# Packing both parts of a split activation into one 512-column matmul, with the halves added at the exit from PSUM

## The chip, the cores and the metric

One NeuronCore of a Trainium2 chip runs the whole program. The metric is the device time of one execution in microseconds (us), as the median of several executions. Three runs of the kernel before took 2057.48, 2062.37 and 2063.44 us. The profiler's names of the engines are used throughout: PE is the tensor engine's matmul, PEld its load of the stationary operand, DVE the vector engine, ACT the scalar engine, POOL the GpSimd engine, SP the engine whose queue issues the loads from memory.

## The reference, cut to what matters

Two blocks of two layers each run over 256 context tokens and 256 latent tokens of width 1024. Each layer has a mixer (an mLSTM with two gated side paths in the first block, attention in the second), an output projection with a gated residual, and a feed-forward part. Where the change acts, this is computed:

```python
x = x + g1 * (y_x @ w_out[l])                          # output projection, residual
x = x + g2 * swiglu(rmsnorm(x, norm2_g[l]) * (1.0 + sc2) + sh2, w_gu[l], w_down[l])

def swiglu(h, w_gu, w_down):
    gate, up = jnp.split(h @ w_gu, 2, axis=-1)
    return (jax.nn.silu(gate) * up) @ w_down
```

All of it is in float32. In the first layer of each block the context tokens go the same way as the latent ones; in the last layer of each block only the latent tokens go on.

## The kernel before, in words

The residual stream lies in eight tiles `xT[k]` of 128 channels by 512 tokens (columns 0 to 255 are context, `CTX`; 256 to 511 are latents, `LAT`). A float32 product is made of three matmuls of a faster kind: a weight W is split in `whi` + `wlo` (an ACT copy at L392, a DVE subtraction at L397), an activation x in `aH` + `aL` (in the feed-forward part `hH` + `hL`), and W.T x is taken as whi·xH + whi·xL + wlo·xH. `mm3` (L411 to L413) issues these three, each with a stationary 128x128 tile of weights and 256 or 512 moving columns (tokens), and all three add up in the same columns of one PSUM bank, a tile of 512 float32 columns per partition. `accA` loops `mm3` over the eight (or 6 and 5) tiles of input channels. In this text the three matmuls for one tile of channels are called a triple.

Products of 512 tokens are those of the feed-forward parts that carry both streams (f0 with d0 in the first block, f2 with d2 in the second; d is the down projection), apart from a few at their heads and tails that go stream by stream (`order`). Products of 256 tokens are all output projections (`part`, called by `out_early`, `out_proj`, `out_stream` and `early_stream`), both parts of the feed-forward for latents alone (f1, d1, f3, d3), and those heads and tails. The products of the input projections are not touched.

What leaves PSUM: in a feed-forward part an ACT Silu reads the gate product `pg` (L557), a DVE multiplication reads the up product `pu` (L558), then the hidden tile is split (ACT and DVE, L378 and L379). In f1 and f3 the first two pairs of products take an input that is not yet normed ("raw", 258 columns) and leave by their own way. An output projection `po` or down projection `pd` leaves by one DVE instruction, x += g * product (`residual`, L454).

The order on each engine is worked out at build time by a scheduler that simulates readiness and follows priorities; on the chip each engine runs its list in order. Weight tiles go through three sets of buffers (five within a feed-forward part), PSUM tiles of products through three banks (five in f1 and f3). Beside the products DVE computes the modulation vectors of later layers, one dot product of 1024 elements per partition at a time (`junk`, L165), paced by `work`: one for each pair of products in f1, none in f3.

## Time and profile before

| what | value |
|---|---|
| runs, us | 2057.48, 2062.37, 2063.44 (median 2062.37) |
| span of the profiled execution, us | 2055.1 (its own time is not listed apart from the runs; the median lies 7.3 above the span) |
| PE busy | 2010.6 us, 98% |
| PEld busy | 1784.5 us, 87% |
| DVE busy | 1545.2 us, 75% |
| ACT busy | 924.5 us, 45% |
| POOL busy | 85.7 us, 4% |
| DMA, mean | 158 GB/s |
| chain that ended last | PE 89%, DVE 6%, ACT 2% |
| mean granted TensorE clock | 0.994 |

A row of PE is pipelined: a matmul's record is longer than the distance to the next one, so durations of PE records don't add up, and the pace is read from how many matmuls start in a stretch. In the rows of groups, "x" is a count, then come the busy time in us and the mean of one in ns. The stages in time: start and first mixer to 266 us, output projections 222 to 311, f0 with d0 to 690, second mixer to 858, f1 with d1 to 1045, attention and its output projections to 1277, f2 with d2 to 1640, attention and its output projection to 1860, f3 with d3 to the end.

### The profile page before, as it was taken

To read this page: it belongs to the slowest core of one execution; us is meant where nothing else is said; L and a number is where in the kernel's file an instruction comes from. 1 tells how busy PE (TensorE), PEld (TensorE's weight loads), DVE (VectorE), ACT (ScalarE), POOL (GpSimd) and SP (SyncE) were. 2 spreads that over 40 slices of the span, in tenths; PEclk is the share of its full clock that TensorE was granted. 3 is DMA by queue.
4 is the path that set the end of the run, shared out by engine and by line. 5 is a ranking of instruction groups with operands and counts; after the bars stand their busy time and mean duration, and the time that the engine had idled before them with its cause. 6 is when DMAs were issued, how large, how long until landed. Compare 5 with 4: busy or idle time off the path is not lost.

```text
span 2055.1 us, 34137 instructions
## 1 busy us (share of the span) xinstructions
PE 2010.6 (98%) x13196; PEld 1784.5 (87%) x13196; DVE 1545.2 (75%) x3105; ACT 924.5 (45%) x1612; POOL 85.7 (4%) x103
## 2 busy tenths in 40 slices
PE   8999999999999899999999999999999999999999
PEld 3798779888888799999998789888888889999999
DVE  6997789987898768987877667777653487788554
ACT  4324544222322346744556675322222266666443
POOL 0000010000001000200100002000000200001000
PEclk9999999999999999999999999999999999999999
DMA  7532265678766332576651015446752231216554
GB/s 295 181 103 92 97 232 176 211 248 295 235 216 198 111 102 94 170 263 212 202 171 61 22 41 186 154 149 223 260 170 71 70 112 64 73 54 224 182 157 134
DMA packets 98182, 324.22 MB, mean 158 GB/s; under 512 B 11418, under 2 KB 14234, under 8 KB 98020
## 3 DMA queue, kind: packets, MB, share of 16 engines
q1 hardware_dynamic: 98020, 322.04, 47.7%
q8 instruction: 104, 1.70, 0.3%
q14 instruction: 58, 0.48, 0.1%
HBM read 320.95 MB, written 1.05 MB: 157 GB/s over the span
## 4 chain that ended last, share of the span: by engine, by line
PE 89%; DVE 6%; ACT 2%; DMA 1%; issue 1%; SPq 0%; POOL 0%; ACTq 0%; POOLq 0%; DVEq 0%
PE pg L411 6%; PE pd L411 6%; PE pd L413 6%; PE pd L412 6%; PE pu L413 6%; PE pg L412 6%; PE pu L412 6%; PE pg L413 6%; PE pu L411 6%; PE pin L411 5%; PE pin L413 5%; PE pin L412 5%; PE pov L1223 2%; PE ptq L1127 2%; DVE wlo L397 1%; PE po L411 1%
## 5 line engine op out<-in xcount | busy, mean ns | idle before, releaser
L392 ACT CAST whi<-wraw 128x1024 fp32r<-128x1024 f32 (+2 forms) x443 | 429.5, 973 | 797.0 <-PE pu L412 188.9
L397 DVE TENSOR_TENSOR wlo<-wraw,whi 128x1024 fp32r<-128x1024 f32 (+2 forms) x443 | 502.5, 1138 | 155.0 <-ACT whi L392 152.3
L165 DVE CUSTOM_DVE_ANT_0 junk<-mw,cv,modb 128x1024 bf16<-128x1024 f32 x272 | 349.6, 1285 | 51.3 <-DMA mw<-in_modw 45.2
L411 PE MATMUL pd<-hH,whi 128*128 128x256 f32 (+1 forms) x748 | 245.4, 328 | 0.0
L412 PE MATMUL pd<-hL,whi 128*128 128x256 f32 (+1 forms) x748 | 245.1, 328 | 0.0
L413 PE MATMUL pd<-hH,wlo 128*128 128x256 f32 (+1 forms) x748 | 244.8, 327 | 0.0
L411 PE MATMUL pg<-aH,whi 128*128 128x256 f32 (+1 forms) x704 | 233.8, 332 | 0.3 <-ACT aH L374 0.3
L413 PE MATMUL pu<-aH,wlo 128*128 128x256 f32 (+1 forms) x704 | 233.5, 332 | 0.3 <-DVE wlo L397 0.3
L412 PE MATMUL pg<-aL,whi 128*128 128x256 f32 (+1 forms) x704 | 233.6, 332 | 0.0
L412 PE MATMUL pu<-aL,whi 128*128 128x256 f32 (+1 forms) x704 | 233.2, 331 | 0.0
L411 PE MATMUL pu<-aH,whi 128*128 128x256 f32 (+1 forms) x704 | 233.2, 331 | 0.0
L413 PE MATMUL pg<-aH,wlo 128*128 128x256 f32 (+1 forms) x704 | 233.2, 331 | 0.0
L412 PEld LDWEIGHTS pd<-hL,whi 128*128 128x128 f32 x748 | 142.2, 190 | 12.2
L411 PEld LDWEIGHTS pd<-hH,whi 128*128 128x128 f32 x748 | 142.4, 190 | 12.0
L413 PEld LDWEIGHTS pd<-hH,wlo 128*128 128x128 f32 x748 | 142.2, 190 | 12.0
L411 PE MATMUL pin<-whi,aH 128*128 128x256 f32 x512 | 150.0, 293 | 1.4 <-ACT aH L374 1.1
L412 PE MATMUL pin<-wlo,aH 128*128 128x256 f32 x512 | 148.0, 289 | 0.0
L413 PE MATMUL pin<-whi,aL 128*128 128x256 f32 x512 | 147.2, 289 | 0.3 <-DVE aL L375 0.2
L411 PEld LDWEIGHTS pg<-aH,whi 128*128 128x128 f32 x704 | 133.7, 190 | 13.2 <-ACT aH L374 0.5
L413 PEld LDWEIGHTS pu<-aH,wlo 128*128 128x128 f32 x704 | 133.7, 190 | 13.1 <-DVE wlo L397 0.5
L413 PEld LDWEIGHTS pg<-aH,wlo 128*128 128x128 f32 x704 | 133.8, 190 | 12.6
L412 PEld LDWEIGHTS pg<-aL,whi 128*128 128x128 f32 x704 | 133.8, 190 | 12.5
(339 smaller groups left out, 4150.8 us busy)
## 6 DMA issues: line engine op xcount, KB each, us to landing
wraw<-in_wgu SPq DMA_DIRECT2D x176, 512.0 KB, 4.4
mw<-in_modw SPq DMA_DIRECT2D x168, 512.0 KB, 4.2
wraw<-in_win SPq DMA_DIRECT2D x92, 512.0 KB, 3.5
wraw<-in_wdn SPq DMA_DIRECT2D x64, 384.0 KB, 3.5
wraw<-in_wout SPq DMA_DIRECT2D x47, 512.0 KB, 3.5
wraw<-in_wdn SPq DMA_DIRECT2D x64, 320.0 KB, 3.4
mn<-in_modn SPq DMA_DIRECT2D x18, 512.0 KB, 5.6
mn<-in_modw SPq DMA_DIRECT2D x6, 512.0 KB, 7.3
```

Source lines behind the costliest of these rows:

```text
L165: r = nc.vector.tensor_tensor_reduce(out=junk, in0=w, in1=self.cv[s], scale=1.0, scalar=self.mb_t[:, 2 * b + l, j:j + 1], op0=ALU.mult, op ...
L392: nc.scalar.copy(out=hi[:, :n], in_=raw[:, :n])
L397: nc.vector.tensor_tensor(out=lo[:, :n], in0=raw[:, :n], in1=hi[:, :n], op=ALU.subtract)
L411: mm(out=out, lhsT=wh, rhs=xh, start=start, stop=False)
L412: mm(out=out, lhsT=wh, rhs=xl, start=False, stop=False)
L413: mm(out=out, lhsT=wl, rhs=xh, start=False, stop=stop)
L1127: nc.tensor.transpose(out=pt[:, h, :], in_=a.bitcast(F32).rearrange("p e d -> p (e d)"), identity=self.ident)
L1223: nc.tensor.matmul(out=po[64 * b:64 * b + 64, e // 2, :], lhsT=vN[:, kc, 64 * g:64 * g + 64], rhs=u["PT"][:, kc, :], start=kc == 0, stop=k ...
```

## The change

`aH[k]` and `aL[k]` become the two halves of one tile `aP[k]` (128 x 2 x 512), `hH` and `hL` of one tile `hP`. For products of 256 tokens a new function `accP` takes, for each tile of channels, one matmul of 512 columns (whi against both parts, side by side in the PSUM tile: xH in columns 0 to 255, xL in 256 to 511) and one of 256 columns (wlo against xH, added to columns 256 to 511). For the last tile of channels the two change places. So the PSUM tile holds two halves whose sum is the product, and each way out of PSUM adds them: `residual` does its DVE instruction twice, once per half, and the feed-forward's exit copies the second half on ACT, adds the first on DVE, and goes on from SBUF. Raw pairs, the very first pair of f0 and f2, and products of 512 tokens stay as they were.

```diff
-        self.aH = [g.tile([128, T], F32R, name=f"aH{k}") for k in range(KT)]
-        self.aL = [g.tile([128, T], F32R, name=f"aL{k}") for k in range(KT)]
+        self.aP = [g.tile([128, 2, T], F32R, name=f"aP{k}") for k in range(KT)]
+        self.aH, self.aL = [[a[:, e, :] for a in self.aP] for e in range(2)]
...
+    def accP(self, out, w, xs, first=True, last=True):
+        mm = self.nc.tensor.matmul
+        n = len(xs)
+        for k, x in enumerate(xs):
+            q = slice(128 * k, 128 * k + 128)
+            big = lambda stop: mm(out=out.rearrange("p (e t) -> p e t", e=2), lhsT=w[0][:, q], rhs=x, start=first and k == 0, stop=stop)
+            small = lambda: mm(out=out[:, 256:512], lhsT=w[1][:, q], rhs=x[:, 0, :], start=False, stop=False)
+            if last and k == n - 1:
+                small()
+                big(True)
+            else:
+                big(False)
+                small()
...
     def residual(self, j, ps, cols, gains):
...
-                r = nc.vector.scalar_tensor_tensor(out=self.xT[j][:, a:b], in0=ps[:, a - c0:b - c0],
-                                                   scalar=gains[s][:, j:j + 1], in1=self.xT[j][:, a:b],
-                                                   op0=ALU.mult, op1=ALU.add)
-                self.fence = r.ins
+                for h in range(2 if c1 - c0 == 256 else 1):
+                    r = nc.vector.scalar_tensor_tensor(out=self.xT[j][:, a:b], in0=ps[:, 256 * h + a - c0:256 * h + b - c0],
+                                                       scalar=gains[s][:, j:j + 1], in1=self.xT[j][:, a:b],
+                                                       op0=ALU.mult, op1=ALU.add)
+                    self.fence = r.ins
...
     def part(self, p, w, ks, cols, first, last):
...
-            self.mm3(p[:, :c1 - c0], w[0][:, q], w[1][:, q], self.aH[k][:, c0:c1], self.aL[k][:, c0:c1],
-                     first and n == 0, last and n == len(ks) - 1)
+            self.accP(p, [a[:, q] for a in w], [self.aP[k][:, :, cols[0]:cols[1]]], first and n == 0, last and n == len(ks) - 1)
...
+                    packed = n == 256 and not raw and (i > 0 or hf > 0)
+                    if packed:
+                        for p, w in zip((pg, pu), ws[i]):
+                            self.accP(p, w, [a[:, :, c0:c1] for a in self.aP])
...
+                    elif packed:
+                        t1, t2 = (sg[:, 256:], h[:, 256:]) if both else [fp.tile([128, 256], F32, tag=nm, name=nm) for nm in ("rg", "ru")]
+                        nc.scalar.copy(out=t1, in_=pg[:, 256:])
+                        nc.vector.tensor_tensor(out=sg[:, :n], in0=pg[:, :n], in1=t1, op=ALU.add)
+                        nc.scalar.activation(out=sg[:, :n], in_=sg[:, :n], func=AF.Silu)
+                        nc.scalar.copy(out=t2, in_=pu[:, 256:])
+                        nc.vector.tensor_tensor(out=h[:, :n], in0=pu[:, :n], in1=t2, op=ALU.add)
+                        nc.vector.tensor_tensor(out=h[:, :n], in0=h[:, :n], in1=sg[:, :n], op=ALU.mult)
...
     def down(self, dns, colsets, gains, hs, pace, skew, after=None):
...
+            packed = c1 - c0 == 256
...
+                if packed:
+                    self.accP(p, ws[j, n], [x[:, :, c0:c1] for x in h], *ends)
```

The change moves instructions too, since the scheduler's list follows from the costs it simulates. Three places show what the lists look like.

PE, in f1, the last two tiles of channels of one up product, before (the numbers behind `aH` and `aL` are those of the tiles of channels):

```order
L411 MATMUL pu<-aH_95,whi 128x256
L412 MATMUL pu<-aL_103,whi 128x256
L413 MATMUL pu<-aH_95,wlo 128x256
L411 MATMUL pu<-aH_96,whi 128x256
L412 MATMUL pu<-aL_104,whi 128x256
L413 MATMUL pu<-aH_96,wlo 128x256
```

and now, with the first tile of the next gate product:

```order
L432 MATMUL pu<-aP_95,whi 128x512
L433 MATMUL pu<-aP_95,wlo 128x256
L433 MATMUL pu<-aP_96,wlo 128x256
L432 MATMUL pu<-aP_96,whi 128x512
L432 MATMUL pg<-aP_89,whi 128x512
L433 MATMUL pg<-aP_89,wlo 128x256
```

Three matmuls of 256 columns became one of 512 and one of 256. Over the whole program the list of PE has 1528 matmuls fewer.

DVE, in f1, before (`wlo` is the split of a weight tile for a later product, `hf` the product of gate and up, `hL` its low part, `junk` a dot product for a later layer's modulation):

```order
L558 TENSOR_TENSOR hf<-pu,sg 128x256
L397 TENSOR_TENSOR wlo<-wraw,whi 128x1024
L379 TENSOR_TENSOR hL_8932<-hf,hH_8921 128x256
L397 TENSOR_TENSOR wlo<-wraw,whi 128x1024
L558 TENSOR_TENSOR hf<-pu,sg 128x256
L397 TENSOR_TENSOR wlo<-wraw,whi 128x1024
L379 TENSOR_TENSOR hL_8933<-hf,hH_8922 128x256
```

and now, over about the same work:

```order
L580 TENSOR_TENSOR hf<-pu,ru 128x256
L397 TENSOR_TENSOR wlo<-wraw,whi 128x1024
L581 TENSOR_TENSOR hf<-hf,sg 128x256
L577 TENSOR_TENSOR sg<-pg,rg 128x256
L397 TENSOR_TENSOR wlo<-wraw,whi 128x1024
L379 TENSOR_TENSOR hP_8560<-hf,hP_8560 128x256
L580 TENSOR_TENSOR hf<-pu,ru 128x256
L581 TENSOR_TENSOR hf<-hf,sg 128x256
L397 TENSOR_TENSOR wlo<-wraw,whi 128x1024
L379 TENSOR_TENSOR hP_8561<-hf,hP_8561 128x256
```

Each pair of products has two more DVE instructions, the additions at L577 and L580, and each waits for an ACT copy of the other half (`rg`, `ru`). The splits of the weights stand about as far ahead as before.

DVE, where the latents' output projection of the first layer overlaps the norm of the context (`xn` and `aL` or `aP` are that norm's tiles, `xT` the residual), before:

```order
L373 SCALAR_TENSOR_TENSOR xn<-xT_83,modA_107,npb 128x256
L373 SCALAR_TENSOR_TENSOR xn<-xT_84,modA_107,npb 128x256
L454 SCALAR_TENSOR_TENSOR xT_85<-po,mod_105,xT_85 128x256
L397 TENSOR_TENSOR wlo<-wraw,whi 128x1024
L375 SCALAR_TENSOR_TENSOR aL_101<-xn,mod_105,aH_93 128x256
L375 SCALAR_TENSOR_TENSOR aL_102<-xn,mod_105,aH_94 128x256
L373 SCALAR_TENSOR_TENSOR xn<-xT_85,modA_107,npb 128x256
L373 SCALAR_TENSOR_TENSOR xn<-xT_86,modA_107,npb 128x256
L454 SCALAR_TENSOR_TENSOR xT_86<-po,mod_105,xT_86 128x256
L397 TENSOR_TENSOR wlo<-wraw,whi 128x1024
```

and now:

```order
L373 SCALAR_TENSOR_TENSOR xn<-xT_85,modA_99,npb 128x256
L373 SCALAR_TENSOR_TENSOR xn<-xT_86,modA_99,npb 128x256
L471 SCALAR_TENSOR_TENSOR xT_84<-po,mod_97,xT_84 128x256
L375 SCALAR_TENSOR_TENSOR aP_95<-xn,mod_97,aP_95 128x256
L375 SCALAR_TENSOR_TENSOR aP_96<-xn,mod_97,aP_96 128x256
L471 SCALAR_TENSOR_TENSOR xT_84<-po,mod_97,xT_84 128x256
L397 TENSOR_TENSOR wlo<-wraw,whi 128x1024 x4
L471 SCALAR_TENSOR_TENSOR xT_85<-po,mod_97,xT_85 128x256 x2
L397 TENSOR_TENSOR wlo<-wraw,whi 128x1024
L471 SCALAR_TENSOR_TENSOR xT_86<-po,mod_97,xT_86 128x256 x2
```

Each residual takes two instructions, and four splits of weights that stood between the norm's instructions now come behind them in a row.

## Rows read from the trace of the kernel before

**Rows 1.** The page, busy time by engine (us, share of the span, instructions).

```profile
span 2055.1 us, 34137 instructions
...
PE 2010.6 (98%) x13196; PEld 1784.5 (87%) x13196; DVE 1545.2 (75%) x3105; ACT 924.5 (45%) x1612; POOL 85.7 (4%) x103
```

**Rows 2.** Stretches of steady matmuls: busy us (count) by engine, clock, DMA share, GB/s.

```profile
340.00:640.00 300.00, 300.00 (x1324) 248.17 (x1323) 260.59 (x389) 83.54 (x108) 3.32 (x2) 1.00 0.73 239
1320.00:1620.00 300.00, 300.00 (x1325) 248.46 (x1324) 172.40 (x245) 79.94 (x105) 4.84 (x4) 1.00 0.52 168
...
900.00:980.00 80.00, 80.00 (x669) 80.00 (x669) 60.37 (x91) 36.20 (x57) 0.00 (x0) 1.00 0.65 215
...
1900.00:2040.00 140.00, 140.00 (x1172) 140.00 (x1171) 74.75 (x95) 60.80 (x89) 0.00 (x0) 1.00 0.57 174
```

**Rows 3.** Groups of PE by shape, whole span: the first matmul of each 256-column triple.

```profile
L411 PE MATMUL pd<-hH,whi 128*128 128x256 f32 x440 | 125.5, 285 | 0.0
...
L411 PE MATMUL pg<-aH,whi 128*128 128x256 f32 x384 | 109.1, 284 | 0.3 <-ACT aH L374 0.3
L411 PE MATMUL po<-aH,whi 128*128 128x256 f32 x376 | 108.8, 293 | 0.7 <-ACT aH L949 0.5
...
L411 PE MATMUL pg<-rawH,whi 128*128 128x258 f32 x32 | 9.2, 289 | 0.0
...
L411 PE MATMUL po<-aH,w 128*128 128x256 f32 x8 | 2.2, 280 | 0.0
```

**Rows 4.** Groups of DVE and ACT by shape, whole span: the exits from PSUM of 256 columns.

```profile
L454 DVE SCALAR_TENSOR_TENSOR xT<-pd,mod,xT 128x256 f32<-128x256 f32 x80 | 36.5, 479 | 37.9 <-PE pd L413 37.9
...
L454 DVE SCALAR_TENSOR_TENSOR xT<-po,mod,xT 128x256 f32<-128x256 f32 x48 | 22.8, 477 | 16.0 <-PE po L413 15.7
...
L511 DVE TENSOR_TENSOR rg<-pg,rb 128x256 f32<-128x256 f32 x4 | 1.7, 414 | 0.0
...
L1241 ACT COPY oN<-pto 128x256 f32<-128x256 f32 x16 | 6.0, 375 | 6.4 <-PE pto L1238 6.3
```

**Rows 5.** Groups of DVE by shape in f1, from 900 to 980 us.

```profile
L397 DVE TENSOR_TENSOR wlo<-wraw,whi 128x1024 fp32r<-128x1024 f32 x24 | 29.4, 1223 | 11.8 <-ACT whi L392 11.7
L165 DVE CUSTOM_DVE_ANT_0 junk<-mw,cv,modb 128x1024 bf16<-128x1024 f32 x14 | 17.9, 1281 | 0.2
L558 DVE TENSOR_TENSOR hf<-pu,sg 128x256 f32<-128x256 f32 x15 | 6.3, 421 | 5.8 <-PE pu L413 5.8
L379 DVE TENSOR_TENSOR hL<-hf,hH 128x256 fp32r<-128x256 f32 x14 | 5.8, 418 | 0.0
```

**Rows 6.** Stretches at the ends of output projections, columns as in rows 2.

```profile
290.00:311.00 21.00, 18.82 (x152) 18.39 (x152) 20.80 (x38) 12.22 (x21) 6.13 (x6) 1.00 0.71 243
835.00:858.00 23.00, 20.84 (x171) 20.37 (x170) 20.75 (x35) 15.73 (x31) 12.22 (x12) 1.00 0.67 219
...
1250.00:1280.00 30.00, 28.64 (x231) 27.75 (x231) 27.09 (x49) 18.03 (x28) 6.61 (x7) 1.00 0.62 215
1830.00:1860.00 30.00, 26.77 (x201) 25.48 (x201) 23.43 (x60) 19.34 (x40) 5.53 (x6) 0.94 0.28 97
```

**Rows 7.** The chain that ended last, residuals on it: start us, length us.

```profile
1265.78 0.40 DVE xT L454
...
1274.54 0.40 DVE xT L454
...
1844.38 0.21 PE po L412
...
1851.87 0.48 DVE xT L454
...
1860.14 0.40 DVE xT L454
...
2051.12 0.48 DVE xT L454
```

More of the change, by code (lines that the diff above doesn't have):

```diff
@@ L453, in residual @@
             if a < b:
-                r = nc.vector.scalar_tensor_tensor(out=self.xT[j][:, a:b], in0=ps[:, a - c0:b - c0],
-                                                   scalar=gains[s][:, j:j + 1], in1=self.xT[j][:, a:b],
-                                                   op0=ALU.mult, op1=ALU.add)
-                self.fence = r.ins
+                for h in range(2 if c1 - c0 == 256 else 1):
[3 more added lines that the diff above has]
+                    self.fence = r.ins
     def part(self, p, w, ks, cols, first, last):
-        c0, c1 = cols
         for n, k in enumerate(ks):
             q = slice(128 * k, 128 * k + 128)
-            self.mm3(p[:, :c1 - c0], w[0][:, q], w[1][:, q], self.aH[k][:, c0:c1], self.aL[k][:, c0:c1],
-                     first and n == 0, last and n == len(ks) - 1)
+            self.accP(p, [a[:, q] for a in w], [self.aP[k][:, :, cols[0]:cols[1]]], first and n == 0, last and n == len(ks) - 1)
     def out_early(self, src, cols, ks):
@@ L531, in ffn @@
                 tg = "" if both else str(hf) + "_"
-                hH = [fp.tile([128, w_h], F32R, tag=f"hH{tg}{i}", name=f"hH{i}") for i in range(HALF)]
-                hL = [fp.tile([128, w_h], F32R, tag=f"hL{tg}{i}", name=f"hL{i}") for i in range(HALF)]
-                hs.append((hH, hL))
+                hP = [fp.tile([128, 2, w_h], F32R, tag=f"hP{tg}{i}", name=f"hP{i}") for i in range(HALF)]
+                hs.append(hP)
                 ws = {}
@@ L543, in ffn @@
                     xs, m, cs = ((rH, rL), 258, (0, 258)) if raw else ((self.aH, self.aL), n, cols)
-                    if i == 0 and hf == 0:
+                    packed = n == 256 and not raw and (i > 0 or hf > 0)
+                    if packed:
+                        for p, w in zip((pg, pu), ws[i]):
+                            self.accP(p, w, [a[:, :, c0:c1] for a in self.aP])
+                    elif i == 0 and hf == 0:
                         self.accA([pg[:, :m], pu[:, :m]], ws[i], xs, cs)
@@ L558, in ffn @@
                         nc.vector.tensor_tensor(out=h[:, :n], in0=pu[:, :n], in1=sg[:, :n], op=ALU.mult)
-                    self.split_plain(h[:, :n], hH[i][:, c0 - off:c1 - off], hL[i][:, c0 - off:c1 - off])
+                    self.split_plain(h[:, :n], *[hP[i][:, e, c0 - off:c1 - off] for e in range(2)])
                     self.work(pace * n / w_h)
                 if both:
-                    self.down([dn[hf]], colsets, gains, [(hH, hL)], pace_d, hf == 1, after)
+                    self.down([dn[hf]], colsets, gains, [hP], pace_d, hf == 1, after)
             if not both:
@@ L580, in down @@
                     ws[j, n] = self.weights(dns[q][j][:, 128 * a:128 * b], 128 * (b - a))
-                H, L = hs[q]
-                self.accA([p[:, :c1 - c0]], [ws[j, n]], (H[a:b], L[a:b]), (c0, c1), n == 0, n == len(todo) - 1)
+                h, ends = hs[q][a:b], (n == 0, n == len(todo) - 1)
+                if packed:
+                    self.accP(p, ws[j, n], [x[:, :, c0:c1] for x in h], *ends)
+                else:
+                    self.accA([p[:, :c1 - c0]], [ws[j, n]], [[x[:, e, :] for x in h] for e in range(2)], (c0, c1), *ends)
             self.residual(j, p, cols, gains)
```

## The prediction

> **What bounds the kernel now.** I read the busy times first: PE is busy for 98% of the span and DVE for 75% [rows 1]. PE's busy time is a modelled one, so I then counted matmuls in stretches that hold one shape only. Where all of them have 512 columns, 1324 and 1325 start in 300 us: 226.5 ns each. Where all have 256 columns, 669 start in 80 us and 1172 in 140 us: 119.5 ns each [rows 2]. The reader is to see two things there. PE never waits in these stretches, though DVE's load differs widely (DVE 60.37 of 80 us in f1, 74.75 of 140 in f3), so PE's own pace is the bound. And twice the columns cost 107 ns more, not twice the time: a matmul costs about 107 ns for each 256 columns and 12.5 ns on top (2 x 119.5 - 226.5) whatever its length. That fixed part is what the change saves. At the ends of the output projections the picture is another one: DVE is busy for 20.80 of 21.00 us in the first layer and 27.09 of 30 us in the third, and PE has gaps [rows 6].
>
> **What is removed.** A triple of 256 columns took 3 x 119.5 = 358.5 ns and would take 226.5 + 119.5 = 346.0, so 12.5 ns go, at every triple that is packed. The counts: 440 triples of down projections, 376 + 8 of output projections, 384 gate and as many up triples [rows 3]. The raw gate triples of f1 and f3 have another shape (258 columns, 32 of them) and are not among the 384; 16 in each of f0 and f2 belong to the first pair and stay. That leaves 352 gate and 352 up triples, in all 440 + 384 + 704 = 1528, the number by which PE's list is shorter. By place:
> - f1, d1, f3, d3: 640 gate and up triples and 352 of the down projections, 992 x 12.5 ns = 12.4 us. PE has no gap there, so I count all of it.
> - Heads and tails of f0, d0, f2, d2: 152 triples, 1.9 us, counted.
> - Output projections: 384 triples, 4.8 us if PE were the bound. Of the six passes, the latents' in the first layer and in the third run with DVE nearly full; there I count nothing. The last one runs partly at the lower of the two clock levels (matmuls of 256 columns start 0.21 us apart [rows 7], which is 256 columns at 1.2 GHz with next to nothing on top, in a stretch with a mean granted clock of 0.94 [rows 6], just after PE had waited through the last attention tile's norm); I count 0.4 us. The other three passes give 192 x 12.5 ns = 2.4 us.
>
> Together 17.1 us. No operand that lies in two pieces occurs among the moving operands before. From below I bound such a matmul by the plain one of 512 columns, 226.5 ns; from above by two matmuls of 256, 239 ns, at which the saving is gone. I take the lower end, because the two pieces are read in one instruction with one load of weights, and the row it is nearest to is the 512-column one.
>
> The Trainium skill ("TensorE: Matmul & The Clock Gate", section "Back-to-back issue gap") speaks against the change: by it the distance is the columns divided by 2.4 GHz and 2.5 ns on top. A triple would then save 2.5 ns and all 1528 of them 3.8 us. The trace has 12.5 in place of 2.5, so I go by the rows.
>
> **What is added.** *The feed-forward exits.* There are 44 packed pairs of products (352 / 8), 40 of them in f1 and f3. Each adds two ACT copies of 256 columns out of PSUM (375 ns, by another copy of that shape) and two DVE additions (414 ns, by the nearest operation with one operand in PSUM) [rows 4]. In f1 a pair takes PE 16 x 358.5 = 5.74 us, of which DVE is busy 60.37 / 80, so 4.33 us; now it is 16 x 346.0 = 5.54 us and DVE 4.33 + 0.83 = 5.16, 93%. Most of that is the weights' splits (1.223 us each) and a dot product of 1.281 us [rows 5]. It fits, barely. In f3, without dot products, DVE goes from 53% to 70%. So I cost the exits at nothing: what covers them is PE's 5.54 us a pair, five PSUM banks and weights split some two pairs ahead. If the cover is gone in f1, what DVE lacks is paid in full, pair by pair (a rival below). ACT has room (36.20 of 80 us [rows 2]).
>
> *The residuals.* Each of the 48 output tiles and of the 24 packed down tiles gets a second DVE instruction of 0.48 us that starts 0.40 us behind the first [rows 4, 7]. Those in the midst of d1 and d3 lie beside PE and cost nothing. On the path lie:
> - the last one of a pass whose result the next stage waits for: o1, both tails of d0 and d2 taken as one each, and the end of the program, where the output leaves behind the second instruction: 4 x 0.48 = 1.9 us;
> - the first layer's latents, DVE 99% busy: 8 x 0.40 = 3.2 us;
> - the third layer's latents: four residuals stand on the chain between 1265 and 1275 us (the first and last are shown): 4 x 0.40 = 1.6 us;
> - the last mixer's projection: three on the chain from 1851 to 1861 us, 3 x 0.40 = 1.2 us [rows 7].
>
> Together 7.9 us. The bounds: 0.5 us if only the program's end counts, and 12.8 + 1.9 = 14.7 if all second instructions of the four latent passes stand on the path. I take the middle because the chain shows some of the residuals there and not all.
>
> *What moves.* The first matmul of a packed product now needs both parts of its input, where it needed the high part only: one DVE instruction later (0.4 us) where a product starts right behind its norm. Only the second pair of f0 and f2 and the first packed one of f1 and f3 stand near such a place, and behind other products; nothing. In the first layer the splits of four weight tiles move behind the context's norm on DVE; that is the passage I have at DVE's full price already. SP's and POOL's work stays as it is.
>
> **The sum.** 17.1 - 7.9 = 9.2 us less than the profiled span of 2055.1: 2045.9. The median of the runs lies 7.3 us above that span, so I forecast 2062.4 - 9.2 = **2053 us**. With the bounds (19.1 less 0.5 at best, 14.7 less 14.7 at worst) this case reaches from 2044 to 2062, most of it from 2046 to 2059.
>
> **The rivals.**
> - *The ends of the projections take nearly all of it.* All four latent passes become DVE-bound. Gain 12.4 + 1.9 + 1.6 (the context's two passes), cost 14.7: 1 us gained, 2061. For it: three of the four stretches have DVE at 90% or more [rows 6]. Against: the chain names only some residuals.
> - *DVE becomes the bound in f1.* DVE's idle time there is mostly spent at the head of its list, on ACT's part of a weight and on PE's product [rows 5], and an instruction that waits holds up those behind it. If that idle time doesn't shrink, each of 20 pairs takes 5.74 + 0.83 us in place of 5.54: the gain of 4.0 us in f1 turns into a loss of 16.6, and the sum is 17.1 - 4.0 - 16.6 - 7.9 = -11.4, **2074**, slower. It decides once a pair needs more than 5.54 us of DVE, waits included. Against: the splits run ahead, so PE doesn't wait for DVE when DVE waits for PE.
> - *The change doesn't save a matmul's fixed part,* since a jump to the second piece of the operand costs what a new matmul did: 0 - 7.9, 2070, slower.
> - *Only 2.5 ns a triple go,* as if the 12.5 ns were tied to the 768 columns and not to the matmuls: 3.4 - 7.9 on the same triples, 2067. This is the time by the skill's rule above; the pace of 226.5 against 119.5 speaks against it.
> - *The ends cost only the last residual.* 17.1 + 1.0 - 0.5, 2045.
>
> **How the numbers follow.** A measurement of this kernel can tell a difference of about 0.3%, 6.2 us, from none. The forecast's case has 0.68, of which 0.60 below 2056.2 and 0.08 above it; the ends taking all 0.13 (same); DVE in f1 0.07 (slower); no saving 0.05 (slower); 2.5 ns 0.03 (same); the cheap ends 0.04 (faster). So faster 0.64, same 0.24, slower 0.12. The range from 2043 to 2066 takes in the forecast's bounds, the cheap ends and the costly ones; it leaves out DVE in f1, the case without a saving and the 2.5 ns, 0.15.
>
> **What would show it.** In the profile after: 1528 matmuls fewer; in f3 a packed pair every 5.54 us, that is 32 matmuls, so some 810 in 140 us with DVE at 70%; in f1 the same pace, with DVE at 90 to 95% and no wait of PE for `wlo`. The spans of f3 with d3 and of f1 with d1 shorter by 6 us each. In 290 to 311 us DVE still full and PE waiting longer for `wlo`. The forecast is wrong if the packed pace in f3 is not near 346 ns a pair of matmuls, if PE waits for DVE within f1, or if the stretches at the ends of the projections grow by more than 8 us in all.

## The result, and the profile after

The changed kernel takes **2072.1 us** (median of 12 runs, 2066.7 to 2076.2) where the kernel before, run beside it on the same chip, took 2061.5: a ratio of **1.0051**, 95% interval 1.0041 to 1.0062. It is slower by some 10.7 us; 2053 us, 9.2 less, had been forecast, and 2072 lies above the range.

The two profiled executions differ by more, 17.8 us (spans 2055.1 and 2072.9), since by their own times (some 1.8 us longer than the spans: 2074.68 for 2072.9) the one before lies 4.6 us below its median and the one after 2.5 above. The page of after, beside [rows 1]:

```profile
span 2072.9 us, 31291 instructions
...
PE 2012.2 (97%) x11668; PEld 1710.9 (83%) x11668; DVE 1602.3 (77%) x3265; ACT 953.2 (46%) x1700; POOL 89.2 (4%) x103
```

PE has 1528 matmuls fewer and yet is busy for 1.6 us more; DVE has 160 instructions and 57 us more. The steady stretches answer to [rows 2], in f1 and in f3 (busy us and count of PE, PEld, DVE, ACT, POOL; clock, DMA share, GB/s):

```profile
920.00:980.00 60.00, 60.00 (x342) 52.19 (x341) 54.82 (x88) 36.16 (x65) 0.00 (x0) 1.00 0.73 241
1900.00:2000.00 100.00, 100.00 (x571) 87.05 (x570) 76.04 (x115) 61.78 (x113) 0.00 (x0) 1.00 0.62 190
```

In both PE never waits: 342 matmuls in 60 us and 571 in 100 us, 175 ns each, so some 351 ns for a pair of one long and one short matmul where 346 were forecast. Starts can be compared exactly from one gate product of f3 to the next, 48 matmuls before and 32 now: 5.760 us before, 5.640 us after, the same to 1 ns in each of 14 distances. A pair of one long and one short matmul thus takes 352.5 ns, and 7.5 ns are saved per triple, not 12.5.

The rest is a loss. I cut both traces at the first matmul of each kind of product (us; "rest" is what the change hardly touches; `e` columns are experiments told below, each one execution; stretches with the same work vary by up to 7 us between executions, see "rest"). The last three lines take together the six stretches other than "rest" and the two that begin with d1 or d3: their length, the time in them in which no matmul's record runs, and the time in them at the lower of PE's two clock levels:

```
stretch                            before   after   e3_inner  e7_two_res  e9_po+inner  e12_pairs
first output projection to d0       205.1   214.2    203.5      216.3       211.5       203.9
second output projection to f1       26.6    24.5     26.6       25.3        24.5        26.9
f1 to d1                            130.7   133.7    128.9      131.4       135.3       126.8
d1 to third output projection       217.5   215.6    215.5      215.5       215.5       214.1
third output projection to d2       202.7   210.1    202.3      207.0       207.5       202.3
last output projection to f3         38.3    38.0     38.3       38.3        37.6        38.3
f3 to d3                            128.8   130.6    125.8      129.7       127.9       126.3
d3 to the last matmul                63.2    62.1     62.1       62.1        62.1        61.8
rest                               1038.4  1039.6   1045.7     1038.9      1039.3      1039.4
six stretches together              732.1   751.2    725.3      748.0       744.4       724.4
  PE idle in them                    12.5    27.2     12.2       20.2        24.2        13.3
  at the lower clock level in them    6.8    37.5      3.4       34.1        30.7         3.4
```

The loss stands where an output projection ends and the feed-forward part begins: 9.1 us in the first layer, 7.4 in the third, 3.1 and 1.8 from the heads of f1 and f3 to their down projections. These last two are net of what packing saves there (320 triples of 7.5 ns, 2.4 us in each), so the heads themselves lose 5.5 and 4.2. The waits of PE show what it waits for (engine, line, what it waited for: us in all, times, longest):

```profile
PE npc L323 <- POOL sqa L347: 6.3, 5, 2.1
...
PE pg L411 <- DVE xT L471: 4.0, 2, 3.2
...
PE po L433 <- DVE wlo L397: 3.9, 4, 1.5
...
PE po L432 <- DVE xT L471: 2.5, 2, 1.3
...
PE pg L412 <- DVE aP L375: 1.7, 2, 1.1
```

Before, no wait for a residual is listed; for `wlo` PE waited once in an output projection, and for `sqa` less:

```profile
PE npc L323 <- POOL sqa L347: 4.1, 4, 1.7
...
PE po L413 <- DVE wlo L397: 1.5, 1, 1.5
```

The waits for residuals of over 1 us all lie in the first layer. In the third PE waits for the norm of f2 (1.5 us for `sqa`, 1.1 for `aP`) and then runs at the lower clock level for 10.2 us. A wait of a *gate* product for a *residual* looks odd, for it reads nothing of it: the product needs a PSUM bank, and the bank still holds an output tile whose second half DVE has not yet taken. The timeline of DVE in the first layer shows why (start us, us, instruction, idle before):

```profile
306.41 0.47 DVE L471 SCALAR_TENSOR_TENSOR xT<-po,mod,xT 128x256 f32<-128x256 f32 x1
...
308.84 0.48 DVE L471 SCALAR_TENSOR_TENSOR xT<-po,mod,xT 128x256 f32<-128x256 f32 x1
309.23 0.87 DVE L375 SCALAR_TENSOR_TENSOR aP<-xn,mod,aP 128x256 fp32r<-128x256 f32 x2
310.02 0.48 DVE L471 SCALAR_TENSOR_TENSOR xT<-po,mod,xT 128x256 f32<-128x256 f32 x1
310.41 4.62 DVE L397 TENSOR_TENSOR wlo<-wraw,whi 128x1024 fp32r<-128x1024 f32 x4
316.79 1.00 DVE L471 SCALAR_TENSOR_TENSOR xT<-po,mod,xT 128x256 f32<-128x256 f32 x2 [1.75 <-PE po L432]
```

and PE beside it:

```profile
307.03 0.47 PE L432 MATMUL po<-aP,whi 128*128 128x512 f32 x1 [1.27 <-DVE xT L471]
...
310.64 0.55 PE L411 MATMUL pg<-aP,whi 128*128 128x256 f32 x1 [3.15 <-DVE xT L471]
...
312.06 0.63 PE L432 MATMUL po<-aP,whi 128*128 128x512 f32 x1
...
312.49 0.41 PE L433 MATMUL po<-aP,wlo 128*128 128x256 f32 x1
...
312.70 0.63 PE L432 MATMUL po<-aP,whi 128*128 128x512 f32 x1
```

This is the list that stands ahead of the prediction: halves of a residual with the norm's instructions between them, then four splits of weights in a row. At 306.41 and at 310.02 DVE does a second half, and only then may PE start (307.03 and 310.64, a little after each). Behind the second wait PE is slow: a long and a short matmul start 0.64 us apart (312.06 to 312.70), where the pair takes 0.353 at the full clock. The granted clock has fallen to the lower of its two levels, 1.2 GHz. The same is seen at the other ends (columns as above; the first line is of before, the others of after):

```profile
300.00:320.00 20.00, 19.56 (x162) 19.34 (x161) 18.09 (x42) 11.71 (x21) 3.65 (x4) 1.00 0.52 176
...
300.00:320.00 20.00, 15.25 (x68) 12.34 (x67) 17.05 (x31) 9.44 (x17) 9.08 (x5) 0.83 0.52 176
310.00:317.00 7.00, 6.09 (x19) 5.15 (x20) 5.25 (x7) 0.59 (x2) 4.47 (x1) 0.53 0.60 180
860.00:880.00 20.00, 16.20 (x111) 15.18 (x111) 16.80 (x33) 11.44 (x23) 6.61 (x7) 0.91 0.62 208
1290.00:1310.00 20.00, 18.51 (x107) 17.30 (x108) 13.60 (x36) 6.37 (x14) 0.00 (x0) 0.83 0.27 80
1860.00:1880.00 20.00, 16.56 (x78) 13.89 (x79) 16.53 (x31) 15.14 (x29) 6.82 (x6) 0.83 0.35 131
```

From 300 to 320 the mean clock is 0.83 where it was 1.00, and PE waits for 4.75 of the 20 us. Over the span the mean is 0.987 in place of 0.994. As an estimate: 1 - 0.994 means that 1.2% of 2055 us ran at half speed, 25 us, and 1 - 0.987 means 2.6% of 2073, 54 us; half of each is lost, so some 15 us of PE's time went that way on top. Not all of it was on the path. The six stretches give a closer account: PE idle for 14.7 us more, and 30.7 us more at half speed. As an estimate, idle time and half of the slow time (where PE isn't idle) make 29.1 us more than before; the stretches are 19.1 us longer, and packing saves 8.2 us in them (1088 triples of 7.5 ns), 27.3 in all. So about half of the loss is PE's waiting and half the lower clock behind the waits.

### The profile page after: what moved, and what is told of

Same layout as the page of the kernel before. It is cut to its first block, busy times and chain, and to the rows that moved or that the text cites. A ratio compares the mean times of both kernels' runs of the same rounds, so it can differ in the third digit from the quotient of the medians.

```text
span 2072.9 us, 31291 instructions
## 1 busy us (share of the span) xinstructions
PE 2012.2 (97%) x11668; PEld 1710.9 (83%) x11668; DVE 1602.3 (77%) x3265; ACT 953.2 (46%) x1700; POOL 89.2 (4%) x103
## 5 line engine op out<-in xcount | busy, mean ns | idle before, releaser
L432 PE MATMUL pd<-hP,whi 128*128 128x512 f32 x440 | 155.5, 398 | 0.7 <-ACT whi L392 0.7
L411 PE MATMUL pin<-whi,aP 128*128 128x256 f32 x512 | 149.7, 293 | 2.0 <-ACT aP L374 1.7
L412 PE MATMUL pin<-wlo,aP 128*128 128x256 f32 x512 | 147.0, 287 | 0.0
L413 PE MATMUL pin<-whi,aP 128*128 128x256 f32 x512 | 146.0, 286 | 1.0 <-DVE aP L375 1.0
L432 PE MATMUL po<-aP,whi 128*128 128x512 f32 x376 | 141.4, 418 | 4.4 <-DVE xT L471 2.5
L411 PE MATMUL pg<-aP,whi 128*128 128x512 f32 (+1 forms) x352 | 134.8, 383 | 4.8 <-DVE xT L471 4.0
L412 PE MATMUL pg<-aP,whi 128*128 128x512 f32 (+1 forms) x352 | 134.9, 383 | 1.7 <-DVE aP L375 1.7
L411 PE MATMUL pu<-aP,whi 128*128 128x512 f32 (+1 forms) x352 | 135.1, 384 | 0.1
L412 PE MATMUL pu<-aP,whi 128*128 128x512 f32 (+1 forms) x352 | 134.8, 383 | 0.0
L413 PE MATMUL pu<-aP,wlo 128*128 128x512 f32 (+1 forms) x352 | 134.7, 383 | 0.0
L413 PE MATMUL pg<-aP,wlo 128*128 128x512 f32 (+1 forms) x352 | 134.3, 382 | 0.0
L432 PE MATMUL pg<-aP,whi 128*128 128x512 f32 x352 | 128.5, 398 | 0.6 <-DVE aP L375 0.6
L432 PE MATMUL pu<-aP,whi 128*128 128x512 f32 x352 | 128.5, 398 | 0.2 <-DVE rgb L528 0.2
L411 PE MATMUL pd<-hP,whi 128*128 128x512 f32 x308 | 119.8, 389 | 0.0
L412 PE MATMUL pd<-hP,whi 128*128 128x512 f32 x308 | 119.8, 389 | 0.0
```

What stands on the lines that cost most here:

```text
L411: mm(out=out, lhsT=wh, rhs=xh, start=start, stop=False)
L412: mm(out=out, lhsT=wh, rhs=xl, start=False, stop=False)
L413: mm(out=out, lhsT=wl, rhs=xh, start=False, stop=stop)
L432: big = lambda stop: mm(out=out.rearrange("p (e t) -> p e t", e=2), lhsT=w[0][:, q], rhs=x, start=first and k == 0, stop=stop)
```

## The experiments

Theory J: the second residuals at the ends of the output projections hold DVE and PSUM banks, PE waits for them, and the clock falls. Rival X: the feed-forward exits load DVE in f1 and f3. The letters in the expectations are these; B, D, O, L and S are explained where they stand, and what e6_grouped calls theory J is another thing, the alternation of the two lengths of matmul. In the diffs, `halves` is a new argument of `residual` that sets how many DVE instructions it takes.

**Which part loses.** e1_po_plain puts the output projections back to triples and one residual, and e2_po_only packs them alone:

```diff
 e1   part():      accP(...)              ->  mm3(...)
      residual(j, p, cols, gains, 1)
 e2   swiglu:      packed = False
      down:        packed = False
```

> The output projections go back to triples and one residual instruction; the feed-forward products stay packed. Theory J (the loss sits at the ends of the output projections: the second residual holds back DVE and PSUM banks, PE waits, and the granted clock falls): the passage from the first output projection to d0 falls from 214 us back to 205, that of the third layer from 210 to 203, and 1144 packed triples that each save 7.4 ns (the pace in the changed kernel's f3, 352.6 ns against 360) leave a gain of some 7 us: about 2054, ratio 0.9965 against before. Theory X (the feed-forward exits load DVE and hold PE in f1 and f3, which grew by 3.1 and 1.8 us up to their down projections): these stretches stay as long as in the changed kernel and the time is about 2064, ratio 1.001.

> Only the output projections are packed; all feed-forward products are triples as before. Theory J: the two long passages grow as in the changed kernel, by 9 and 7 us, and nothing is gained elsewhere: about 2074, ratio 1.006. Theory X: the projections alone cost little more than their second residuals, about 2065, ratio 1.002.

Measured: e1_po_plain 2056.5 us, ratio to before 0.9974 (0.9962 to 0.9986); e2_po_only 2073.1, 1.0065 (1.0051 to 1.0079). The packed output projections by themselves cost more than the whole change, and without them the change is a small gain. With them plain, f1 takes 129.9 us and f3 126.3 up to their down projections, less than before (130.7 and 128.8), with all the exits in place: X falls. J's part of the loss in f1 and f3 is real too: in e2_po_only, where f1 and f3 are plain, they took 134.3 and 132.0.

**Only where PE never waits.** e3_inner packs f1, d1, f3 and d3 alone, without the heads and tails of f0, d0, f2 and d2:

```diff
-                    packed = n == 256 and not raw and (i > 0 or hf > 0)
+                    packed = n == 256 and not raw and not both
-            packed = c1 - c0 == 256
+            packed = not both
```

> Packed are only the products of f1, d1, f3 and d3 (992 triples, 40 pairs with the new exit); heads and tails of f0, d0, f2, d2 and all output projections are as before. Theory J: 992 x 7.4 ns = 7.3 us gained less 0.5 us at the end: about 2054.5, ratio 0.9967. Theory X: f1 and f3 up to their down projections are 4 to 5 us longer in place of shorter, about 2064, ratio 1.001.

Measured: 2052.7 us, ratio 0.9962 (0.9949 to 0.9974): faster than both kernels. 992 triples at 7.5 ns make 7.4 us; it gained some 8. Its interval overlaps that of e1_po_plain, so what the heads and tails cost stays unsettled: the forecast has them gain 0.9 us, and e1_po_plain, which packs them, lies 2.5 us above e3_inner by the ratios.

**The second residual or the packed matmul.** Four kernels make a square over e3_inner: output projections as triples or packed, one residual instruction or two. e7_two_residuals has triples and a second instruction that multiplies by 0; e8_one_residual is packed and takes the first half alone, so that its sum lacks the second half (xL's and wlo's products); e9_po_and_inner has both.

```diff
 e7   second instruction:  in0=ps[:, same columns], scalar=0.0
 e8   residual(j, p, cols, gains, 1)      with accP in part()
 e9   residual(j, p, cols, gains, 2)      with accP in part()
```

> As e3_inner, with the output projections as triples, but each 256-column residual of an output projection is followed by a second DVE instruction of the same shape that reads the same PSUM columns again, times 0, and adds nothing. PE's work is that of e3_inner. Theory J says: the second residual, which holds DVE and the PSUM tile longer, is the whole loss, so the time rises from e3_inner's 2052.7 by 10 to 18 us, with PE waits for DVE's xT and lower granted clock at the ends of the output projections. Rival: the loss comes from the packed matmuls' order on PE (the first matmul of a product needs both parts of its input); then the time stays within 4 us of e3_inner.

> As e3_inner, with the output projections packed, but their residual adds the first half of the PSUM tile alone, in one DVE instruction: the second half (xL's and wlo's products) is left out of the sum. PE's work is that of the change. Theory J says: without a second residual there is no loss, and 384 triples at 6 to 7 ns each go, so the time is 2049 to 2054 us, no PE waits for xT at the ends. Rival (the order on PE): the time rises by 8 us or more over e3_inner.

> As e3_inner with the output projections packed and both halves added by the two residuals, the fourth corner beside e3_inner, e7_two_residuals and e8_one_residual. From the change without its heads and tails (which cost 3 to 4 us between e1_po_plain and e3_inner): some 2068 us. Theory J says that it lies near e7_two_residuals less 2 to 3 us; the rival, that it lies near e8_one_residual.

| output projections | one residual | two residuals |
|---|---|---|
| triples | e3_inner 2052.7, 0.9962 (0.9949 to 0.9974) | e7_two_residuals 2070.7, 1.0047 (1.0034 to 1.0060) |
| packed | e8_one_residual 2058.2, 0.9984 (0.9970 to 0.9999) | e9_po_and_inner 2066.5, 1.0029 (1.0016 to 1.0043) |

Second residuals alone cost 18 us over triples, with PE's matmuls untouched, and 8.2 over packed products. In e7_two_residuals these are 48 instructions (group by shape; then two of PE's waits, and the clock in the first layer):

```profile
L471 DVE SCALAR_TENSOR_TENSOR xT<-po,xT 128x256 f32<-128x256 f32 x48 | 20.0, 418 | 0.3
```

```profile
PE po L411 <- DVE xT L471: 4.3, 4, 2.2
...
PE po L413 <- DVE wlo L397: 3.3, 2, 2.2
```

```profile
310.00:320.00 10.00, 9.08 (x61) 9.08 (x62) 6.95 (x9) 2.94 (x4) 5.09 (x3) 0.75 0.55 192
```

20 us of DVE's time and 18 us of the kernel's are near each other, but that is no proof that each second residual is paid in full. The first layer, with 16 of the 48 (6.7 us of DVE), is 12.9 us longer than in e3_inner, and the stretch from the second output projection to f1 is 1.3 us shorter. In the six stretches PE is idle for 8.0 us more and at the lower clock level for 30.7 us more, so that by the estimate above about two thirds of the loss is the clock and one third the waits. J's forecast for e7_two_residuals is met at its upper end (10 to 18 us), and the pure form of its rival, that the order on PE does it all, falls. But J's figure for e8_one_residual (2049 to 2054) was missed: packing the projections without a second residual is slower than e3_inner by 5.5 us, not faster, and the rival's 8 us is missed as well. DVE has as many instructions there as in e3_inner, 3201, so this part comes from PE's new products or from the order of the lists, and no run takes these two apart. The stretch from f1 to d1 shows where half of it is: 131.7 us against 128.9. The start of f1 in e8_one_residual,

```profile
852.75 0.39 PE L432 MATMUL po<-aP,whi 128*128 128x512 f32 x1
855.58 0.59 PE L323 MATMUL npc<-ones,sqa 128*128 128x1 f32 x2 [2.44 <-POOL sqa L347]
...
857.04 0.42 PE L412 MATMUL pu<-rawL,whi 128*128 128x258 f32 x1
857.25 0.42 PE L413 MATMUL pu<-rawH,wlo 128*128 128x258 f32 x1
```

and in e3_inner,

```profile
853.17 0.28 PE L413 MATMUL po<-aP,wlo 128*128 128x256 f32 x1
854.35 0.38 PE L323 MATMUL npc<-ones,sqa 128*128 128x1 f32 x2 [0.90 <-POOL sqa L347]
...
854.80 0.28 PE L412 MATMUL pg<-rawL,whi 128*128 128x258 f32 x1
854.92 0.29 PE L413 MATMUL pg<-rawH,wlo 128*128 128x258 f32 x1
```

The norm's sum is late in e8_one_residual, PE waits 2.44 us in place of 0.90, and behind the longer wait matmuls start 0.21 us apart, at the lower clock level, where they start 0.12 apart behind the shorter one. The two effects don't add up (5.5 and 18.0 apart, 13.8 together): each kernel has lists of its own. From e9_po_and_inner to the change, which has the heads and tails as well, it is another 4.5 us by the ratios, again with intervals that overlap. Both comparisons point the same way, and in both the stretch of the first layer grows (from 203.5 to 206.9 us in e1_po_plain, from 211.5 to 214.2 in the change): heads and tails seem to cost something where a gain was forecast, but how much isn't shown.

**DVE's time, the PSUM bank, or the order.** e10_sbuf_second is e7_two_residuals with a second instruction that leaves PSUM alone; e11_priority is e9_po_and_inner with the residuals ahead of the norm in the scheduler's list.

```diff
 e10  second instruction:  in0=self.xT[j][:, a:b], scalar=0.0
 e11  + with self.tc.high_priority(offset=400):   around the residual's instructions
```

> As e7_two_residuals (2070.7 us), but the second DVE instruction of each output projection's residual reads its own xT in SBUF, times 0, in place of the PSUM tile: as many DVE instructions in nearly the same order, while the PSUM tile is free after the first. Theory B (the PSUM tile is held longer): PE's waits for DVE's xT go and the time falls to 2053 to 2058 us, near e3_inner (2052.7). Theory D (DVE's list itself: its length, and the order in which it stands): the time stays at 2066 to 2071, as in e7_two_residuals.

> As e9_po_and_inner (2066.5 us: output projections packed, two residuals), but the residuals stand in the scheduler's list with a priority 400 steps higher, so in DVE's list of the first layer they come before the norm of the context and in the midst of the splits of weights, where without the second residual (e3_inner) they stood. DVE's work is the same. Theory O (the order of DVE's list, which the second residuals upset): the time falls to 2053 to 2060 us, and the waits for xT go. Theory L (the length of DVE's work there): it stays within 3 us of 2066.5, with the waits moved to another place.

Measured: e10_sbuf_second 2075.0 us, 1.0069 (1.0056 to 1.0081); e11_priority 2070.5, 1.0049 (1.0035 to 1.0062). Theory B falls: with the bank free after the first instruction PE's waits for `xT` fall from 4.3 to 1.0 us, but the time is no better. It lies even above theory D's 2066 to 2071, with second instructions that take 2.0 us more of DVE in all. PE waits for the splits that stand behind on DVE (its waits of e10_sbuf_second, then the second instructions' group):

```profile
PE po L413 <- DVE wlo L397: 6.1, 3, 3.8
```

```profile
L471 DVE SCALAR_TENSOR_TENSOR xT<-xT 128x256 f32<-128x256 f32 x48 | 22.0, 463 | 0.3
```

Theory O's forecast (2053 to 2060) fails too: this other order doesn't bring the time back. Theory L allowed 3 us beside e9_po_and_inner's 2066.5, and it is 4, with intervals that overlap. With the residuals ahead, no wait of 3 us for `xT` is left, but PE waits for `wlo` and, at the head of f3, for the norm, which now stands behind them (e11_priority):

```profile
PE po L433 <- DVE wlo L397: 4.1, 4, 1.5
...
PE pg L432 <- DVE aP L375: 3.4, 2, 3.2
```

So neither a free bank nor this one other order brings the time back. What e7_two_residuals, e9_po_and_inner, e10_sbuf_second and e11_priority have in common is the length of DVE's work between the last output tile and the first products of the feed-forward part: residuals, splits and norm all have to be done there, and PE waits for whichever stands last. That reading fits all four, but it is argued and not shown: no run takes other work off DVE there. In all four the second instruction also writes `xT`, so the norm starts later; that alone, at 0.40 to 0.48 us for each of six passes, would be under 3 us as an estimate. And e8_one_residual shows that something else costs time as well.

How the loss divides into waits and clock differs from kernel to kernel. In the six stretches of e11_priority PE is idle for 24.0 us, 11.8 more than in e3_inner, and at the lower clock level for 17.1 us, 13.7 more; here the waits are the larger part. The mean clock of an execution hides this: it is 0.992 in e11_priority and 0.991 in e3_inner, whose slow stretches lie elsewhere.

**The pace.** In the change the long matmul of f1 and f3 starts 224 to 241 ns ahead of the short one, and the short one 113 to 120 ns ahead of the next long one; before, 512 columns took 226.7 and 256 columns 120.0. Is it the operand in two pieces, or the two lengths in turn? e5_both512 makes the second matmul as long as the first (it adds wlo times xL to the sum), e6_grouped and e12_pairs issue equal lengths in a row on e3_inner's base:

```diff
 e5   small: out[:, 256:512], rhs=x[:, 0, :]      ->  out (2 x 256), rhs=x
 e6   accP: all long ones but the last, then all short ones, then the last long one
 e12  the same over the gate and the up product together: 7 + 7 long, 8 + 8 short, 1 + 1 long
```

> The packed products' second matmul takes 512 columns as well (the low part of the weights against both parts of the input; it adds the product of the two low parts, which the reference's float32 product has and the kernel before left out). What makes a pair of 512 and 256 columns take 352.6 ns and not 346.7: if it is that matmuls of two lengths alternate, all matmuls of a packed product now start 226.7 ns apart, as in the plain products of 512 columns (a pair 453 ns, d3 176 x 453 = 79.8 us); if it is the reading of both parts, or the weights changing at each matmul, they start about 235 ns apart (a pair 470 ns, d3 82.7 us).

> As e3_inner (packed only in the inner parts of f1, d1, f3 and d3; 2052.7 us), but within a packed product all matmuls of 512 columns come first and then all of 256, the last of 512 at the end. Theory J says: what the packed pace lacks (352 ns for a pair of matmuls where 346 were forecast) is due to the alternation of the two lengths, so the pair comes down to 346 or 347 ns, and the 992 triples' places save another 5 to 6 us: some 2047 us, f3's and f1's gate and up products shorter by some 2 us each, d1 and d3 by 1 us each. Rival: the loss per pair lies in the packed matmul itself, in where its operand lies, and the pace and the time stay as in e3_inner (2052.7).

> As e6_grouped (2048.5 us; there 5.587 us from one gate product of f3 to the next, that is a gate and an up product, where 5.640 in the change and 5.547 at 120.0 and 226.7 ns without any loss), but grouped over both products of a pair in f1 and f3: the first seven matmuls of 512 columns of the gate, then of the up product, then all sixteen of 256 columns, then the last of 512 of each. Theory S (each change of length costs a fixed amount, about 20 ns for a change forth and back): half as many changes, so 5.567 us a pair and 2047.5 to 2048 us in all, which the total can't tell from e6_grouped but the pairs can. Rival (the rest of the loss lies in the products themselves, in the tiles that they read): 5.587 us a pair as before.

The windows in f3, of e5_both512, of e3_inner, of e6_grouped and of e12_pairs:

```profile
2000.00:2100.00 100.00, 100.00 (x443) 82.79 (x442) 55.98 (x83) 47.15 (x84) 0.00 (x0) 1.00 0.45 143
```

```profile
1880.00:1980.00 100.00, 100.00 (x569) 87.01 (x568) 75.34 (x117) 61.96 (x113) 0.00 (x0) 1.00 0.56 185
```

```profile
1880.00:1980.00 100.00, 100.00 (x576) 88.06 (x575) 73.78 (x112) 61.19 (x112) 0.00 (x0) 1.00 0.58 185
```

```profile
1880.00:1980.00 100.00, 100.00 (x579) 88.51 (x578) 67.41 (x110) 57.74 (x109) 0.00 (x0) 1.00 0.57 182
```

In e5_both512 (2207.4 us, a single run) a gate and an up product of f3 together take 7.253 us, 32 times 226.7 ns: the operand in two pieces costs nothing there. The lengths in turn do. In e6_grouped the first five or so long matmuls behind a group of short ones start 228 to 236 ns apart, and only then 226.7 is reached; the first short one behind the long ones is early by 7. A change of length forth and back costs some 20 ns. A long and a short matmul take 349.2 ns together, and not the 346 or 347 of the expectation. Gate to gate in f3:

| | changes of length forth and back in a pair of products | us |
|---|---|---|
| before (triples) | 0 | 5.760 |
| the change, e3_inner | 14 | 5.640 |
| e6_grouped | 2 | 5.587 |
| e12_pairs | 1 | 5.567 |
| 16 x (226.7 + 120.0) ns, worked out | 0 | 5.547 |

From e6_grouped to e12_pairs one change less takes off 20 ns, and the last one stands for the 20 that remain: theory S, in the figure that it gave. With changes in every pair of matmuls each costs less, (5.640 - 5.547) / 14 = 6.6 ns, for the pace never settles. One thing stays open: in d3 of e5_both512, where all lengths are equal, the products over the first half of the hidden tiles still alternate between 237 and 229 ns, and those over the second half take 226.7. So something other than the length slows matmuls there, and grouping gains little in d3: 61.7 us in e6_grouped against 62.1 in e3_inner, where 1 us less was expected.

In time, e6_grouped took 2048.5 us, 0.9941 (0.9922 to 0.9960), and **e12_pairs 2047.1, 0.9940 (0.9927 to 0.9954)**, the fastest of all: 0.6% below before. The two can't be told apart by the total; by the pairs they can.

## Why the prediction was wrong

**What was right.** PE's own pace is the bound inside f1, f3 and d3, and in f3 the operand in two pieces runs at the plain pace, the lower end that I took. The feed-forward exits are hidden: in f1 DVE is busy 54.82 of 60 us, 91% where 90 to 95% was forecast, and PE doesn't wait. The groups of f1, beside [rows 5], show the additions at 422 ns, near the 414 assumed:

```profile
L397 DVE TENSOR_TENSOR wlo<-wraw,whi 128x1024 fp32r<-128x1024 f32 x22 | 26.9, 1221 | 2.4 <-ACT whi L392 2.1
...
L580 DVE TENSOR_TENSOR hf<-pu,ru 128x256 f32<-128x256 f32 x11 | 4.6, 423 | 2.0 <-ACT ru L579 2.0
...
L577 DVE TENSOR_TENSOR sg<-pg,rg 128x256 f32<-128x256 f32 x10 | 4.2, 422 | 0.9 <-ACT rg L576 0.8
```

DVE's idle time before these instructions, 17.6 of 80 us in [rows 5], shrank to 5.3 of 60, as the argument against the rival "DVE in f1" said. In f3 DVE is at 76% where 70% was said. The last residual costs 0.5 us at the end of the program:

```profile
2068.44 0.49 DVE xT L471
2068.96 0.48 DVE xT L471
```

**The step that failed first: "together 7.9 us" for the second residuals.** Of these, 6.5 us were those of the output projections (3.2 + 1.6 + 1.2, and 0.5 for o1), and with 2.8 us gained on PE packing them was to cost 3.7 us net. It costs 13 to 16: by the ratios 13.4 us from before to e2_po_only, 13.8 from e3_inner to e9_po_and_inner, 15.9 from e1_po_plain to the change. With the 2.9 us that PE saves there (384 x 7.5 ns) that is 16 to 19 us of cost, more than even the upper bound of 14.7, which was "all second instructions of the four latent passes on the path". How much of it is the second instruction depends on the kernel around it: 18.0 us over triples in e7_two_residuals (12 to 23 by the ends of both intervals), 8.2 from e8_one_residual to e9_po_and_inner. The bound priced DVE's own time and not what follows from it: PE waits, and its wait ends in a stretch at the lower clock level, 0.64 us for a pair of matmuls in place of 0.353; the clock is about half of the loss in the six stretches. And the bound ended at the last output tile, whereas the DVE work that is late there is the next stage's: the heads of f1 and f3 lose 5.5 and 4.2 us, and the third layer's 7.4 us are lost behind the first gate product of f2 (131.0 us from there to d2 in place of 122.9).

**The step that hid it: "that is the passage I have at DVE's full price already".** The order showed the four splits behind the norm and the halves of a residual torn apart. I read that as the same DVE work in another order. It was the place where PE came to wait 3.15 us for a bank and then for `wlo`. In e11_priority, with one other order, PE waits for the splits and the norm instead, and the time is no better; whether some third order would be isn't known.

**The term that was mis-sized: "12.5 ns go, at every triple that is packed".** It is 7.5. On the places counted that makes 10.3 us, not 17.1. The step took the pace of long matmuls among long ones and of short ones among short ones [rows 2]; the rows had no stretch in which the two lengths alternate, and I bounded the operand in two pieces and not the alternation. The fixed part is as large as I took it, even 13.3 ns (2 x 120.0 - 226.7; the 119.5 came from counting in a window, which takes in two or so matmuls that had started ahead of it), and e12_pairs gets 12.1 of it back, (5.760 - 5.567) / 16. The Trainium skill's rule ("TensorE: Matmul & The Clock Gate", section "Back-to-back issue gap", 2.5 ns on top of the columns, given for isolated matmuls) doesn't hold for these rows either: 120.0 ns for 256 columns at 2.4 GHz is 13.3 ns on top.

**d1** was to gain 2.2 us and lost 0.2 (64.0 to the end of its matmuls before, 64.2 after). DVE is busy for 19.55 of its first 20 us, and PE waits 0.7 us there for a weight's `whi`. e6_grouped has d1 at 62.4.

**The sum again, by parts,** each measured by the ratios to before:

| part | forecast, us | measured, us |
|---|---|---|
| f1, d1, f3, d3 and the end of the program | -12.4 + 0.5 = -11.9 | e3_inner: -7.8 |
| output projections | -2.8 + 6.5 = +3.7 | from e3_inner to e9_po_and_inner: +13.8 |
| heads and tails of f0, d0, f2, d2 | -1.9 + 1.0 = -0.9 | from e9_po_and_inner to the change: +4.5, not clear of noise |
| together | -9.2 | +10.5 |

Of the three signs that the prediction gave of being wrong, the last came true beyond doubt: the stretches at the ends of the projections grew by 14.1 us in all (9.1 - 2.1 + 7.4 - 0.3). Of the rivals, "the ends of the projections take nearly all of it" named the place; its price, like the bound, stopped at DVE's own time. The two whose times lie nearest to 2072, "no saving" (2070) and "DVE in f1" (2074), are near by luck: a triple does save 7.5 ns, and PE doesn't wait for DVE in the steady part of f1.

## What to carry to other kernels

An operation that PE saves may have to be paid for on the engine that empties PSUM: compare the two in the stretch where that engine is fullest, not in the mean, and let the bound include the wait of PE and the slower clock behind it. Where DVE was full between two stages, 48 added instructions of 0.42 to 0.48 us cost 8 to 22 us here, and neither a free PSUM bank nor the other order that was tried won them back. Pack matmuls where the pace is PE's own, keep equal lengths together, and leave the rest alone: that part alone was 0.6% faster than before.

## What had not been expected of the hardware

- The pace of matmuls in f1 and f3 depends on their neighbours' length: 226.7 ns for 512 columns and 120.0 for 256 among their like, some 20 ns lost at a change of length forth and back, and 228 to 236 ns for the first five or so long ones behind short ones. Length isn't all: half of d3 in e5_both512 runs at 229 and 237 ns with equal lengths.
- Two waits of PE of like kind end differently: behind 0.90 us the next matmuls of 258 columns start 0.12 us apart, behind 2.44 us 0.21 us apart (e3_inner and e8_one_residual, one execution each).
- A DVE instruction that reads both operands from SBUF was not the cheaper one: 463 ns in e10_sbuf_second against 418 in e7_two_residuals, where one operand came from PSUM, and 478 to 480 where a scalar per partition was read as well. Why is not shown.
